# Bringing the experts' rows back through a table in DRAM in place of selection matmuls, for 12 of 16 pairs of experts

## The chip, the core and the metric

The kernel runs on one core of a Trainium2 chip. Its engines are named as in the profile: PE (TensorE, the matmuls), DVE (VectorE), ACT (ScalarE), POOL (GpSimd) and SP (SyncE, which here only issues transfers). The core's 16 DMA engines are shared by all queues. The metric is the device time of one execution in microseconds, as the median of several runs.

## The reference

Two layers of a decoder trunk, on 256 tokens of 1024 columns, all in f32. Each layer has four token mixers whose outputs are gated, projected and added to the residual, and then a hierarchical mixture of experts. This is the part that matters here:

```python
lc = (xf @ w_coarse) + b_coarse                 # 4 groups
grp = jnp.argmax(lc, axis=-1)
p_grp = jnp.take_along_axis(jax.nn.softmax(lc, axis=-1), grp[:, None], axis=-1)
lf = ((xf @ w_fine) + b_fine).reshape(N, 4, 8)  # 8 experts a group
lf = jnp.take_along_axis(lf, grp[:, None, None], axis=1)[:, 0]
top_p, top_e = lax.top_k(jax.nn.softmax(lf, axis=-1), 2)
wts = p_grp * top_p / jnp.sum(top_p, axis=-1, keepdims=True)
eid = grp[:, None] * 8 + top_e
moe = routed_experts(xf, eid, wts, w13, w2)     # sum over a token's two experts of
                                                # wts * (silu(x w1) * (x w3)) w2
x = x + g2 * moe
```

So each of the 256 tokens goes to two of 32 experts, 512 token-and-expert rows in all, and a token's result is the sum of two weighted rows and the residual. An expert's matrices are w13 (1024 x 512, w1 and w3 side by side) and w2 (256 x 1024).

## The kernel before, in words

Everything is one program for one core, two layers one after the other. All compute instructions are recorded through one helper, so they carry one line number (L253); the profile tells them apart by the names of the tiles. The order of each engine's instructions is fixed when the program is written: the mixers by a hand-made order of units (SEQ, KEYS) with a rough clock that fills TensorE's waits, the experts by the plain loop of `experts`.

Tiles in SBUF: `ring` are 8 tiles of 1 MB for weights, `pg` a pool of pages of 128 x 1024 f32 (512 KB; 29 of them, for weights too, w2 above all), `gt`, `sm` and `smb` smaller scratch, `K` the table of constants with the identity. PSUM banks are `at` (short-lived) and `mm` (long sums). The weights of the whole program are one stream of pieces in a fixed order, issued by SyncE at L320 (`advance`), as soon as `done` has given back a ring tile or a page.

A layer's experts go by pairs: 16 pairs, each expert with 64 slots for its tokens, so a pair has 128 slots, one per partition. `route` gives `rk`, for each token and expert its place among the expert's tokens. The loop over p from 0 to 15 does, for pair p:

1. `first(p)`: 32 matmuls of the pair's gathered columns (XG) with w13, then SwiGLU on ScalarE and VectorE (`swiglu`: a tanh, two VectorE operations).
2. `scatter` of pair p-1: eight matmuls `mm<-pg 128x512` of the transposed selection (ST, zeros and ones, slots by tokens) with the pair's weighted rows, which add them to the four long-lived banks `acc` (256 tokens by 1024 columns).
3. `prep_g`: gathers for the pairs to come, also by selection matmuls (`at<-pg 128x256`).
4. `hidden_t(p)`: two transposes of the hidden rows (`at<-K,gt`), copied to SBUF by ScalarE.
5. In odd pairs `prep_t` for the next two pairs: `selection_t` (four transposes `at<-K,pg`, the ST of `scatter`) and `slot_weights` (`at<-W,pg 128x4`, the weight of each slot).
6. `second(p)`: matmuls of the hidden rows with w2 (`at<-pg,gt`) into two banks, each weighted by `weighted`: VectorE multiplies by the slot's weight and the gate, and `split` makes two fp32r parts for the scatter (ScalarE copies, VectorE subtracts).

The sum `acc` is started before routing by `seeds(0)` and `seeds(1)`: each two matmuls of the identity with the residual X, in f32 (four passes), `mm<-pg,K`. After pair 15 come `more_rounds` (a branch, taken only if an expert has more than 64 tokens), the last scatter, the copy of `acc` to X, and in the last layer the output.

Of the kernel before, what the change touches and what calls it, by code (L numbers as in the profile page):

```python
# [31 lines left out]
# columns of the table of shape constants  # L32
C_ID, C_IOTA, C_EI, C_SL, C_TABLES, C_TRI, C_N = 0, 128, 192, 224, 230, 1190, 1318
# [16 lines left out]
def shape_constants():  # L50
    import numpy as np
    k = np.zeros((128, C_N), np.float32)
    tab = k[:, C_TABLES:C_TRI]
    p = np.arange(128)[:, None]
    c = np.arange(256)[None, :]
    k[:, C_ID:C_ID + 128] = np.eye(128)
    dist = 128 + p - c
    tab[:, C_DM:C_DM + 256] = np.where(dist >= 0, dist, BIG)
    tab[:, C_DW:C_DW + 256] = np.where((dist >= 0) & (dist < 128), dist, BIG)
    tab[:, C_MK:C_MK + 256] = np.where(dist >= 0, 0.0, -1e30)  # L60
    t = np.arange(S).reshape(2, 128).T
# [12 lines left out]
    k[:, C_TRI:C_TRI + 128] = np.arange(128)[:, None] < np.arange(128)[None, :]  # L74
    k[:, C_IOTA:C_IOTA + 64] = np.arange(64)[None, :]
    k[:, C_EI:C_EI + 32] = np.arange(32)[None, :]
    return k


# the order of the units of each layer before its experts  # L80
# [27 lines left out]
# the order of their weights  # L108
# [20 lines left out]
class Clock:  # L129
    '''a rough forecast, while the program is written, of when each engine gets through with what it has been given'''  # L130
# [18 lines left out]
    def known(self, a, t):  # L149
        '''the tile's content is written by t'''  # L150
# [27 lines left out]
    def cost(self, e, name, out, ins):  # L178
# [6 lines left out]
        if e == "P":  # L185
# [9 lines left out]
            # strips of the array work side by side  # L195
# [63 lines left out]
def kernel(ctx, tc, x_in, c_in, w_ada, b_ada, norm_gain, w_in, qk_gain, cmp_pe, cmp_w1, cmp_w2,  # L259
# [9 lines left out]
    ps = ctx.enter_context(tc.tile_pool(name="ps", bufs=1, space=bass.MemoryType.PSUM))  # L269
    ctx.enter_context(tc.manual_schedule())  # L270
# [70 lines left out]
    def two(key, n, src, off, row, tag="any"):  # L341
        '''rows of n columns, in one piece of the ring or in two pages'''
# [76 lines left out]
    def load_rest():  # L419
# [13 lines left out]
        A.dma_start(tri_f, consts[:, C_TRI:C_TRI + 128])  # L433

    ID = K[:, C_ID:C_ID + 128]
    one = cst.tile([128, 1], FT, name="one")
# [17 lines left out]
    def slopes(l):  # L454
        # gains of the queries, in units of each head's slope
# [14 lines left out]
    def rsqrt(ss, n, inv, eng=None):  # L470
        '''1 / sqrt(ss * inv + EPS): a guess from the exponent, a step of third order and one of Newton's'''
# [34 lines left out]
    strips = cst.tile([128, 2], FT, name="strips")  # L506
# [5 lines left out]
    four = cst.tile([128, 1], FT, name="four")  # L512
# [4 lines left out]
    def put(l, part, src):  # L517
        '''eight columns of a shift or a scale, with their bias'''
# [10 lines left out]
    def strip_columns(r, rows, p=None):  # L529
        '''the sums of some strips, as columns'''  # L530
# [5 lines left out]
    def ada_pe(l, part):  # L536
        '''1024 columns on the tensor engine: two blocks of columns by even and odd rows of 128, in four strips'''
# [35 lines left out]
    def ada_v(l, part, pool=False):  # L573
        '''1024 columns, the products by row summed on the vector engine, the rows by the tensor engine'''
# [44 lines left out]
    def gate_tile(l):  # L619
        # the bias goes in as a row  # L620
# [4 lines left out]
    def router_bias(l):  # L625
        # the router's bias carries the shift through the router's weights
# [33 lines left out]
    # the residual's rows turned to columns while their norms are worked out  # L660
# [57 lines left out]
    # where the columns go: the first and the last, the tile, its columns  # L718
# [25 lines left out]
    # the first columns: the residual times the gain's scale; the norm and the shift come in afterwards  # L744
# [94 lines left out]
    # the output projection: halves of the columns (n) by halves of the rows (f)  # L839
# [43 lines left out]
    def prep(raw, n, groups):  # L883
        '''per-head RMS normalisation of n raw heads; groups: (raw column, heads, copies, column in the result)'''
# [21 lines left out]
    def pairs(xn, col, n, dst, gain):  # L906
        '''n blocks of 128 columns, transposed, times a gain by row'''
# [10 lines left out]
    def scores(qf, kf, i):  # L918
        # the two heads of a pair may lie in different rows of the array, so each has a bank
# [7 lines left out]
    def biased(p, i, slopes, table):  # L927
        '''the scores, negated, and the negated largest of each row'''
# [29 lines left out]
    def attend(qf, kf, vf, slopes, table, take, gate=None, sinks=None):  # L958
        '''four heads by twos, each pair's output turned, as heads by tokens'''
# [47 lines left out]
        def one_pair(i):  # L1007
            # a number that is yielded: the banks that the next step takes; held: those that are read later
# [9 lines left out]
    def turned(b):  # L1018
        '''takes a branch's output for the projection'''
# [29 lines left out]
    def g_nsa(l):  # L1049
# [3 lines left out]
        # the raw keys and values of the compressed branch, twice side by side  # L1053
# [40 lines left out]
    def compressed(l, kT2, qT, gg, oa):  # L1094
        # hidden layer of the compression: keys and values, by halves of the hidden units
# [274 lines left out]
    # the engine of each part of the modulation: six parts a layer  # L1370
# [111 lines left out]
    def mixers(l):  # L1482
# [34 lines left out]
        def when():  # L1517
            '''when the next filling unit can start, None if not before something else is written'''
# [9 lines left out]
        def aside(force):  # L1528
            '''one of the units beside, if it is its turn'''
# [253 lines left out]
    def residual1(l, c0, c1, acc):  # L1783
        '''some columns of the residual, and their squares'''
# [9 lines left out]
    def router_part(l, q):  # L1794
        '''a quarter of the rows of the router's product'''
# [29 lines left out]
    def route(l, rs, lo):  # L1825
        '''group by its largest logit, two experts of it, and each token's place among its expert's tokens'''
# [3 lines left out]
        ei = K[:, C_EI:C_EI + 32]  # L1830
# [24 lines left out]
        # zeros and ones, exact in any type  # L1855
# [9 lines left out]
        # weights, off the path to the gather  # L1865
# [10 lines left out]
        def further():  # L1876
            # how many further rounds of CAP rows each pair of experts needs
# [7 lines left out]
        def weights():  # L1885
            V.tensor_reduce(den, ec, axis=AX.X, op=OP.add)
# [29 lines left out]
    def slot_weights(sel, ws, n):  # L1916
        p = at([128, n // 2, 2, 2])
# [5 lines left out]
        for e in range(2):  # L1923
            V.tensor_reduce(w[64 * e:64 * e + 64], p[64 * e:64 * e + 64, :, :, e], axis=AX.X, op=OP.add)
# [44 lines left out]
    def scatter(acc, st, ys, last):  # L1969
        for n in range(2):  # L1970
            for t in range(2):
                for j in range(2):
                    T.matmul(acc[t][n], st[:, 128 * t:128 * t + 128], ys[n][:, j], start=False, stop=last and j == 1)

    def more_rounds(l, acc):
        tot = nc.values_load(NRt[0:1, 16:17], min_val=0, max_val=3)
        with tc.If(tot > 0):
            with tc.For_i(0, NE // 2) as pi:
# [3 lines left out]
                V.tensor_copy(wsl, W[:, :, :, ds(2 * pi, 2)])  # L1982
# [32 lines left out]
    def experts(l):  # L2015
# [6 lines left out]
        # the sum of the experts starts from the residual  # L2022
        acc = {}
# [8 lines left out]
        seeds(0)  # L2032
# [22 lines left out]
        seeds(1)  # L2055

        NP = NE // 2
        SEL, ST, SW, XG = {}, {}, {}, {}
# [26 lines left out]
        def second(p, gT):  # L2085
            ys = []
            for n in range(2):
# [6 lines left out]
                ys.append(weighted(y, SW[p // 2][:, p % 2:p % 2 + 1], MOD[l, "g2"][:, 512 * n:512 * n + 512]))  # L2094
# [14 lines left out]
        for p in range(NP):  # L2109
# [7 lines left out]
            if l + 1 < DEPTH and p == NP - 1:  # L2117
                tables()
            g = first(p)
# [3 lines left out]
            else:  # L2123
                scatter(acc, ST[(p - 1) // 2][:, (p - 1) % 2], ys, False)
# [8 lines left out]
            ys = second(p, gT)  # L2133
        more_rounds(l, acc)
        scatter(acc, ST[q][:, i], ys, True)
# [72 lines left out]
```

## Time and profile before

| what | value |
|---|---|
| median of 3 runs | 1083.64 us (1081.47 to 1084.21) |
| span of the profiled execution | 1081.6 us |
| TensorE busy | 1039.9 us, 96% |
| VectorE, ScalarE, GpSimd busy | 55%, 41%, 13% |
| moved by DMA | 337.5 MB, mean 312 GB/s; written to HBM 1.05 MB |
| experts of layer 0 (first half of pair 0 to the last scatter) | about 311 to 552 us |
| experts of layer 1 | about 836 to 1076 us |

The profiled execution's span lies 2.0 us below the median of the runs. A timeline row gives the start from the span's beginning, the duration of a run of like instructions, engine, operation, tiles and count, and in brackets the idle time in front and what ended it. A duration of several matmuls includes the pipeline's tail, so the time that a group holds the engine is read from its start to the start of the next. DMA issues on SyncE are short; a long one is a row of several issues that waited for a tile in between.

### The profile page before, as it was taken

What the parts mean: (1) busy time and instruction counts of PE and PEld (TensorE: products, weight loads), DVE (VectorE), ACT (ScalarE), POOL (GpSimd) and SP (SyncE); (2) the same over time, 40 slices, a digit from 0 to 9 for tenths busy, and PEclk for the clock granted to TensorE, in tenths of its full rate; (3) what the DMA queues carried; (4) which work ended last, traced back from release to release, by engine and by line L of the source; (5) the groups of instructions that cost most, each with busy time, mean ns of one, the idle gap of its engine ahead of it and who ended that gap; (6) DMA issues with size and microseconds to landing.
All of it is one profiled execution on the core that took longest, in us unless ns stands there. A gap on an engine that the chain in (4) does not pass through costs nothing. (4 is left out here: it accounts for less than half of the span.)

```text
span 1081.6 us, 15476 instructions
## 1 busy us (share of the span) xinstructions
PE 1039.9 (96%) x5615; PEld 657.2 (61%) x5616; DVE 597.3 (55%) x1316; ACT 444.0 (41%) x1089; POOL 136.4 (13%) x273
## 2 busy tenths in 40 slices
PE   5989999999999999999999989999999999999997
PEld 3567777787854455544447867778876554555542
DVE  2656678888553333333357875986876233333332
ACT  2554857654441222222146467666444222221211
POOL 0021443320010000000001342530201000000000
PEclk8999999999999999999999999999999999999999
DMA  9977765678899999999966784556779799999991
GB/s 353 401 256 271 264 206 198 216 273 311 309 350 362 409 353 410 411 412 412 413 236 238 277 332 140 195 195 246 285 276 364 275 406 346 411 411 410 412 397 40
DMA packets 151056, 337.50 MB, mean 312 GB/s; under 512 B 13196, under 2 KB 30908, under 8 KB 150972
## 3 DMA queue, kind: packets, MB, share of 16 engines
q1 hardware_dynamic: 144166, 334.66, 82.2%
q10 hardware_dynamic: 6678, 1.77, 0.7%
q8 instruction: 46, 0.75, 0.3%
q14 instruction: 38, 0.31, 0.1%
q0 software_dynamic: 128, 0.02, 0.0%
HBM read 335.36 MB, written 1.05 MB: 311 GB/s over the span
## 5 line engine op out<-in xcount | busy, mean ns | idle before, releaser
L253 PE MATMUL mm<-pg 128*128 128x512 f32 (+4 forms) x1984 | 468.9, 388 | 8.5 <-ACT pg L253 7.1
L253 PEld LDWEIGHTS mm<-pg 128*128 128x128 f32 x1984 | 352.7, 189 | 120.7 <-issue 34.7
L253 PE MATMUL at<-ring,pg 128*64 128x512 f32 (+2 forms) x912 | 242.7, 569 | 2.4 <-POOL pg L253 2.4
L253 PE MATMUL at<-pg 128*128 128x256 f32 (+6 forms) x1192 | 226.6, 363 | 3.2 <-ACT pg L253 2.1
L253 DVE TENSOR_TENSOR pg<-ring,pg 128x512 fp32r<-128x512 f32 (+4 forms) x276 | 182.0, 695 | 68.2 <-ACT pg L253 66.2
L253 PEld LDWEIGHTS at<-pg 128*128 128x128 f32 (+3 forms) x1192 | 130.4, 167 | 71.3 <-issue 57.4
L253 ACT ACTIVATE pg<-ring 128x512 fp32r<-128x512 f32 (+4 forms) x276 | 148.7, 602 | 17.9 <-DMA rbs<-in_b_fine_dram 5.1
L253 PEld LDWEIGHTS at<-ring,pg 128*64 128x64 f32 (+2 forms) x912 | 81.1, 137 | 101.4 <-issue 88.7
L253 PE MATMUL at<-pg,gt 128*64 128x512 f32 x512 | 116.9, 598 | 2.2 <-ACT gt L253 2.1
L253 ACT ACTIVATE gt<-at 128x256 f32<-128x256 f32 x64 | 24.6, 384 | 213.6 <-PE at L253 213.6
L253 DVE SCALAR_TENSOR_TENSOR gt<-gt,at 128x256 f32<-128x256 f32 x32 | 13.5, 421 | 147.2 <-ACT gt L253 147.2
L253 ACT ACTIVATE pg<-gt 128x512 fp32r<-128x512 f32 x64 | 40.3, 629 | 115.5 <-DVE gt L253 115.5
L253 DVE SCALAR_TENSOR_TENSOR gt<-at,sm,pg 128x512 f32<-128x512 f32 x64 | 47.9, 748 | 61.8 <-PE at L253 61.8
L253 ACT ACTIVATE pg<-pg,sm 128x128 f32<-128x128 f32 (+2 forms) x168 | 70.2, 459 | 17.0 <-DVE sm L253 12.0
L253 ACT ACTIVATE pg<-at 128x512 f32<-128x512 f32 (+5 forms) x106 | 49.9, 503 | 54.9 <-PE at L253 54.7
L253 PEld LDWEIGHTS at<-pg,gt 128*64 128x64 f32 x512 | 33.9, 136 | 60.1 <-issue 52.0
L253 DVE TENSOR_TENSOR pg<-gt,pg 128x512 fp32r<-128x512 f32 x64 | 44.3, 692 | 45.8 <-ACT pg L253 45.1
L253 DVE TENSOR_SCALAR pg<-at,A,mod 128x256 f32<-128x256 f32 x64 | 31.6, 539 | 60.9 <-PE at L253 59.2
L253 PE MATMUL at<-K,pg 128*128 128x128 f32 (+1 forms) x388 | 59.6, 283 | 5.9 <-DVE pg L253 3.4
L253 PEld LDWEIGHTS at<-K,pg 128*128 128x128 f32 (+1 forms) x388 | 46.3, 143 | 20.5 <-DVE pg L253 5.7
L253 DVE SCALAR_TENSOR_TENSOR pg<-ring,cs,pg 128x1024 f32<-128x1024 f32 x44 | 58.0, 1319 | 0.1
L253 ACT ACTIVATE gt<-mm 128x512 f32<-128x512 f32 x44 | 24.5, 594 | 80.9 <-PE mm L253 80.8
(162 smaller groups left out, 676.9 us busy)
## 6 DMA issues: line engine op xcount, KB each, us to landing
pg<-in_w_dram SPq DMA_DIRECT2D x196, 512.0 KB, 11.0
ring<-in_w_dram SPq DMA_DIRECT2D x94, 1024.0 KB, 12.1
ring<-in_w_ada_dram SPq DMA_DIRECT2D x45, 1024.0 KB, 7.8
ring<-in_w_in_dram SPq DMA_DIRECT2D x33, 1024.0 KB, 4.7
ring<-in_cmp_w_dram SPq DMA_DIRECT2D x8, 1024.0 KB, 6.4
ring<-in_w_branch_dram SPq DMA_DIRECT2D x8, 1024.0 KB, 4.9
ring<-in_w_out_dram SPq DMA_DIRECT2D x8, 1024.0 KB, 5.0
ring<-in_w_in_dram SPq DMA_DIRECT2D x8, 976.0 KB
```

The costliest lines, as they stand in the source:

```text
L253: return f(*args, **kw)
```

## The change

`NSUM = 4`: only the last four pairs (12 to 15) are still summed by selection matmuls. For pairs 0 to 11 `second` weights both halves straight into one page y1 (128 slots by 1024 columns), without the split, and `put_rows` sends the page by an indirect DMA from GpSimd's queue to a table in DRAM, one of 512 rows by 1024 columns for each layer. Row 2 * token + choice belongs to a token's first or second expert. The row of each slot comes from a third part of W, which rides along in `slot_weights` (now 128x6) and is made an integer by two VectorE operations; empty slots get row 1024, which is out of bounds and dropped.

At pair 14 `fetch` reads the table back into four pages of 512 KB by GpSimd's queue, at pair 15 `gather_rows` adds the two rows of each token (four GpSimd additions) and adds them to X (two VectorE additions). The seeds now come after the second half of pair 15 and add that X to `acc`; the sum is started by the first of the scatters left, which is that of pair 12. Rows that no pair below 12 writes must be zero, so both tables are zeroed once, by two ScalarE DMAs of 2 MB (from one zeroed tile of 128x512) while the parameters are loaded. The constants lose a table of 32 columns and gain two; some small tiles share one (`few`).

```diff
+NROW, NOROW = 512, 1024
+NSUM = 4
...
+    rows_of = [dr.tile([NROW, D], FT, name=f"rows{l}") for l in range(DEPTH)]
...
+        zero = T_("gt", [128, 512])
+        G.memset(zero, 0.0)
+        for r in rows_of:
+            A.dma_start(r.rearrange("(p r) (a c) -> p (r a) c", p=128, c=512),
+                        zero[:, None, :].to_broadcast([128, 8, 512]))
...
-    W = cst.tile([128, 2, 2, NE], FR, name="W")
+    W = cst.tile([128, 2, 3, NE], FR, name="W")
...
         def weights():
+            for t in range(2):
+                V.tensor_scalar(W[:, t, 2], o12[:, t, 1], K[:, C_ROW + t:C_ROW + t + 1], None, op0=OP.add)
...
+            if rows is not None:
+                V.tensor_scalar(rows[64 * e:64 * e + 64], p[64 * e:64 * e + 64, :, 2, e], float(NOROW), None, op0=OP.add)
...
+    def put_rows(l, y, rows):
+        nc.gpsimd.indirect_dma_start(out=rows_of[l][:, :], out_offset=bass.IndirectOffsetOnAxis(ap=rows, axis=0), in_=y,
+                                     in_offset=None, bounds_check=NROW - 1, oob_is_err=False)
...
-        def seeds(t):
-            acc[t] = [mmb(), mmb()]
-            for n in range(2):
-                T.matmul(acc[t][n], ID, X[t][:, 512 * n:512 * n + 512], start=True, stop=False)
+        def fetch():
+            for t in range(2):
+                for c in range(2):
+                    back[t, c] = pg([128, D])
+                    G.dma_start(back[t, c], rows_of[l].rearrange("(t p c) d -> t c p d", t=2, c=2)[t, c])
+        def gather_rows():
+            for t in range(2):
+                for n in range(2):
+                    c = slice(512 * n, 512 * n + 512)
+                    G.tensor_tensor(back[t, 0][:, c], back[t, 0][:, c], back[t, 1][:, c], op=OP.add)
+                V.tensor_tensor(X[t], X[t], back[t, 0], op=OP.add)
+        def seeds():
+            for t in range(2):
+                for n in range(2):
+                    T.matmul(acc[t][n], ID, X[t][:, 512 * n:512 * n + 512], start=False, stop=False)
...
-            selection_t(SEL[q], ST[q], 4)
-            SW[q] = slot_weights(SEL[q], W[:, :, :, 4 * q:4 * q + 4], 4)
+            if 2 * q + 1 >= SUM:
+                selection_t(SEL[q], ST[q], 4)
+            TO[q] = T_("sm", [128, 2], I32)
+            SW[q] = slot_weights(SEL[q], W[:, :, :, 4 * q:4 * q + 4], 4, TO[q])
...
-                ys.append(weighted(y, SW[p // 2][:, p % 2:p % 2 + 1], MOD[l, "g2"][:, 512 * n:512 * n + 512]))
+                if p < SUM:
+                    V.scalar_tensor_tensor(y1[:, 512 * n:512 * n + 512], y, w, gate, op0=OP.mult, op1=OP.mult)
+                else:
+                    ys.append(weighted(y, w, gate))
+            if p < SUM:
+                put_rows(l, y1, TO[q][:, i:i + 1])
...
+            if p == SUM + 2:
+                fetch()
...
-            else:
-                scatter(acc, ST[(p - 1) // 2][:, (p - 1) % 2], ys, False)
+            elif p > SUM:
...
+                scatter(acc, ST[(p - 1) // 2][:, (p - 1) % 2], ys, p == SUM + 1, False)
+            if p == NP - 1:
+                gather_rows()
...
+        seeds()
         more_rounds(l, acc)
-        scatter(acc, ST[q][:, i], ys, True)
+        scatter(acc, ST[q][:, i], ys, False, True)
```

On TensorE, this is pair 9 of layer 0 before, from its scatter (of pair 8) to the first matmuls of pair 10; `at<-ring,pg` is `first`, `at<-pg,gt` is `second`:

```order
305 L253 MATMUL mm<-pg 128x512 x8
306 L253 MATMUL at<-pg 128x256 x8
307 L253 MATMUL at<-K,gt 128x128 x2
308 L253 MATMUL at<-K,pg 128x128 x4
309 L253 MATMUL at<-W,pg 128x4 x4
310 L253 MATMUL at<-pg,gt 64x512 x8
311 L253 MATMUL at<-ring,pg 64x512 x8
```

And the same pair now:

```order
290 L257 MATMUL at<-pg 128x256 x8
291 L257 MATMUL at<-K,gt 128x128 x2
292 L257 MATMUL at<-W,pg 128x6 x4
293 L257 MATMUL at<-pg,gt 64x512 x8
294 L257 MATMUL at<-ring,pg 64x512 x8
```

The scatter and the selection's transposes are gone, slot_weights is wider by two columns, and the hidden rows' transposes stand one gather behind the first half.

The end of layer 0's experts on TensorE before, pair 15 from the scatter of pair 14 on; `NRt` belongs to `more_rounds`:

```order
390 L253 MATMUL mm<-pg 128x512 x8
391 L253 MATMUL at<-K,gt 128x128 x2
392 L253 MATMUL at<-pg,gt 64x512 x8
393 L1976 TENSOR_LOAD NRt
394 L1977 COMPARE_AND_BRANCH
```

And now:

```order
370 L257 MATMUL mm<-pg 128x512 x8
371 L257 MATMUL at<-K,gt 128x128 x2
372 L257 MATMUL at<-pg,gt 64x512 x8
373 L257 MATMUL mm<-pg,K 128x512 x4
374 L2000 TENSOR_LOAD NRt
375 L2001 COMPARE_AND_BRANCH
```

The scatter of pair 14 stays, and the four seed matmuls stand between the second half of pair 15 and the branch.

On GpSimd, the instructions between layer 0's routing (the last small `sm` operations) and the branch after pair 15, before:

```order
93 L253 TENSOR_TENSOR sm<-smb,sm 128x8
94 L253 TENSOR_TENSOR sm<-sm 128x2
95 L1976 TENSOR_LOAD NRt
96 L1977 COMPARE_AND_BRANCH
97 L1978 COMPARE_AND_BRANCH
```

And now, with the table under its number in the program (`rows_66`):

```order
94 L257 TENSOR_TENSOR sm<-smb,sm 128x8
95 L257 TENSOR_TENSOR sm<-sm 128x2
96 L1994 DMA rows_66<-pg,sm 512x1024 x12
97 L2053 DMA pg<-rows_66 128x1024 x4
98 L257 TENSOR_TENSOR pg<-pg 128x512 x4
99 L2000 TENSOR_LOAD NRt
100 L2001 COMPARE_AND_BRANCH
```

Where the queue went from routing to the branch with nothing between, it now has the twelve puts, the four fetches and the four additions, in this order.

## Rows read from the trace of the kernel before

**Rows 1.** Page: busy time of each engine, and GpSimd's DMA queue.

```profile
PE 1039.9 (96%) x5615; PEld 657.2 (61%) x5616; DVE 597.3 (55%) x1316; ACT 444.0 (41%) x1089; POOL 136.4 (13%) x273
...
q0 software_dynamic: 128, 0.02, 0.0%
```

**Rows 2.** Stretches: length; busy of PE, PEld, DVE, ACT, POOL; clock; DMA share; GB/s.

```profile
70.00:90.00 20.00, 20.00 (x116) 13.93 (x115) 10.25 (x22) 8.49 (x21) 4.24 (x14) 1.00 1.04 373
100.00:120.00 20.00, 19.57 (x167) 13.72 (x165) 12.53 (x39) 12.33 (x47) 6.77 (x24) 1.00 0.78 286
310.00:350.00 40.00, 39.42 (x205) 18.93 (x204) 14.41 (x33) 10.14 (x21) 0.00 (x0) 1.00 0.93 347
380.00:400.00 20.00, 19.97 (x113) 11.03 (x113) 6.37 (x13) 4.83 (x10) 0.00 (x0) 1.00 0.95 334
420.00:530.00 110.00, 110.00 (x569) 54.13 (x564) 36.43 (x73) 22.73 (x45) 0.00 (x0) 1.00 1.04 411
840.00:860.00 20.00, 20.00 (x106) 9.93 (x103) 5.79 (x12) 5.44 (x11) 0.00 (x0) 1.00 0.73 253
900.00:920.00 20.00, 20.00 (x104) 10.16 (x101) 5.47 (x10) 4.34 (x9) 0.00 (x0) 1.00 0.86 322
920.00:1040.00 120.00, 120.00 (x625) 59.88 (x624) 41.02 (x80) 26.30 (x52) 0.00 (x0) 1.00 1.04 411
```

**Rows 3.** Timeline, TensorE, pairs 7 to 9: start, us, operation, count.

```profile
424.25 2.14 PE L253 MATMUL mm<-pg 128*128 128x512 f32 x8
426.22 1.10 PE L253 MATMUL at<-pg 128*128 128x256 f32 x8
427.16 0.38 PE L253 MATMUL at<-K,gt 128*128 128x128 f32 x2
427.38 0.60 PE L253 MATMUL at<-K,pg 128*128 128x128 f32 x4
427.74 0.59 PE L253 MATMUL at<-W,pg 128*128 128x4 f32 x4
...
454.27 0.98 PE L253 MATMUL mm<-pg 128*128 128x512 f32 x3
```

**Rows 4.** Timeline, SyncE's queue in both layers' experts.

```profile
413.16 1.84 SPq L320 DMA_DIRECT2D ring<-in_w_dram  x2
...
505.12 2.42 SPq L320 DMA_DIRECT2D ring<-in_w_dram  x2
...
514.77 4.82 SPq L320 DMA_DIRECT2D pg<-in_w_dram  x4
...
1039.12 4.31 SPq L320 DMA_DIRECT2D pg<-in_w_dram  x4
```

**Rows 5.** DMA issues: tile, queue, count, KB each, us to landing.

```profile
pg<-in_w_dram SPq DMA_DIRECT2D x196, 512.0 KB, 11.0
...
out_dram<-pg SPq DMA_DIRECT2D x4, 256.0 KB, 2.4
...
pg<-in_b_ada_dram POOLq DMA_DIRECT2D x4, 4.0 KB, 5.4
```

**Rows 6.** Timeline, TensorE: last second half of each layer; idle in brackets.

```profile
544.96 3.65 PE L253 MATMUL at<-pg,gt 128*64 128x512 f32 x16 [0.53 <-ACT gt L253]
...
1068.97 3.65 PE L253 MATMUL at<-pg,gt 128*64 128x512 f32 x16 [0.53 <-ACT gt L253]
```

**Rows 7.** Timeline, TensorE, first of the two seeds in layer 0.

```profile
297.24 1.88 PE L253 MATMUL mm<-pg,K 128*128 128x512 f32 x4
```

**Rows 8.** Timeline, VectorE: last step of SwiGLU in pair 7.

```profile
425.23 0.42 DVE L253 TENSOR_TENSOR gt<-gt,at 128x256 f32<-128x256 f32 x1
```

**Rows 9.** Groups of GpSimd's instructions, by form: its additions of 128x512.

```profile
L253 POOL TENSOR_TENSOR pg<-pg,gt 128x512 f32<-128x512 f32 x16 | 29.6, 1875 | 108.4 <-DVE gt L253 108.4
```

**Rows 10.** TensorE after a long idle time, and the stretch at half rate.

```profile
63.48 5.84 PE L253 MATMUL mm<-pg 128*128 128x488 f32 x18 [2.92 <-ACT pg L253]
...
65.00:68.50 3.50, 3.50 (x11) 2.84 (x9) 2.76 (x8) 3.48 (x8) 0.00 (x0) 0.51 1.14 331
```

More of the change, by code (lines that the diff above doesn't have):

```diff
@@ L30 @@
 GATE0 = 2476
-C_ID, C_IOTA, C_EI, C_SL, C_TABLES, C_TRI, C_N = 0, 128, 192, 224, 230, 1190, 1318
+C_ID, C_IOTA, C_SL, C_ROW, C_TABLES, C_TRI, C_N = 0, 128, 192, 198, 200, 1160, 1288
 C_DM, C_DW, C_MK, C_CM, C_VIS, C_COS, C_SIN = 0, 256, 512, 768, 832, 896, 928
@@ L75, in shape_constants @@
     k[:, C_IOTA:C_IOTA + 64] = np.arange(64)[None, :]
-    k[:, C_EI:C_EI + 32] = np.arange(32)[None, :]
+    k[:, C_ROW:C_ROW + 2] = 2 * t - NOROW
     return k
@@ L269 @@
     ps = ctx.enter_context(tc.tile_pool(name="ps", bufs=1, space=bass.MemoryType.PSUM))
+    dr = ctx.enter_context(tc.tile_pool(name="dr", bufs=1, space=bass.MemoryType.DRAM))
+    rows_of = [dr.tile([NROW, D], FT, name=f"rows{l}") for l in range(DEPTH)]
     ctx.enter_context(tc.manual_schedule())
@@ L433, in load_rest @@
         A.dma_start(tri_f, consts[:, C_TRI:C_TRI + 128])
+        zero = T_("gt", [128, 512])
[3 more added lines that the diff above has]
+                        zero[:, None, :].to_broadcast([128, 8, 512]))
+        M.unread.discard(zero.tensor.name)
+        M.used[zero.tensor.name] = M.t["G"] + 20.0
     ID = K[:, C_ID:C_ID + 128]
-    one = cst.tile([128, 1], FT, name="one")
+    few = cst.tile([128, 4], FT, name="few")
+    one, strips, four = few[:, 0:1], few[:, 1:3], few[:, 3:4]
     V.memset(one, 1.0)
@@ L505 @@
     MOD = {}
-    strips = cst.tile([128, 2], FT, name="strips")
     V.tensor_tensor(strips, ID[:, 0:64:32], ID[:, 64:128:32], op=OP.add)
@@ L511 @@
         V.tensor_tensor(evens[:, 32 * i:32 * i + 32], ID[:, 64 * i:64 * i + 32], ID[:, 64 * i + 32:64 * i + 64], op=OP.add)
-    four = cst.tile([128, 1], FT, name="four")
     V.tensor_tensor(four, strips[:, 0:1], strips[:, 1:2], op=OP.add)
@@ L1829, in route @@
             V.scalar_tensor_tensor(L[:, t], H["lg"][t], rs[:, t:t + 1], MOD[l, "rb"], op0=OP.mult, op1=OP.add)
-        ei = K[:, C_EI:C_EI + 32]
+        ei = K[:, C_IOTA:C_IOTA + 32]
         lf = L[:, :, 8:40].rearrange("p t (g e) -> p t g e", g=4)
@@ L1914, in selection_t, with slot_weights @@
         A.activation(st, p, AF.Copy)
-    def slot_weights(sel, ws, n):
-        p = at([128, n // 2, 2, 2])
+    def slot_weights(sel, ws, n, rows=None):
+        p = at([128, n // 2, ws.shape[2], 2])
         for i in range(n // 2):
@@ L1967, in weighted, with scatter @@
         return y
-    def scatter(acc, st, ys, last):
+    def scatter(acc, st, ys, first, last):
         for n in range(2):
@@ L1972, in scatter @@
                 for j in range(2):
-                    T.matmul(acc[t][n], st[:, 128 * t:128 * t + 128], ys[n][:, j], start=False, stop=last and j == 1)
+                    T.matmul(acc[t][n], st[:, 128 * t:128 * t + 128], ys[n][:, j], start=first and j == 0,
+                             stop=last and j == 1)
+    def put_rows(l, y, rows):
+        nc.gpsimd.indirect_dma_start(out=rows_of[l][:, :], out_offset=bass.IndirectOffsetOnAxis(ap=rows, axis=0), in_=y,
+                                     in_offset=None, bounds_check=NROW - 1, oob_is_err=False)
+        M.unread.discard(y.tensor.name)
+        M.used[y.tensor.name] = M.t["V"] + 4.0
     def more_rounds(l, acc):
@@ L1981, in more_rounds @@
                 wsl = T_("sm", [128, 2, 2, 2], FR)
-                V.tensor_copy(wsl, W[:, :, :, ds(2 * pi, 2)])
+                V.tensor_copy(wsl, W[:, :, 0:2, ds(2 * pi, 2)])
                 rounds = nc.values_load(NRt[0:1, ds(pi, 1)], min_val=0, max_val=3)
@@ L2020, in filler @@
                 units.pop(0)[1]()
-        acc = {}
-        def seeds(t):
-            acc[t] = [mmb(), mmb()]
-            for n in range(2):
-                T.matmul(acc[t][n], ID, X[t][:, 512 * n:512 * n + 512], start=True, stop=False)
+        acc, back = {}, {}
+        def fetch():
[13 more added lines that the diff above has]
+                    T.matmul(acc[t][n], ID, X[t][:, 512 * n:512 * n + 512], start=False, stop=False)
         filler(1)
         mm = router_part(l, 3)
-        seeds(0)
         rs = rstd_of(H["ss"])
@@ L2054, in experts @@
         filler(FILL)
-        seeds(1)
         NP = NE // 2
-        SEL, ST, SW, XG = {}, {}, {}, {}
+        SUM = NP - NSUM
+        SEL, ST, SW, XG, TO = {}, {}, {}, {}, {}
         def prep_sel(q):
@@ L2086, in second @@
             ys = []
+            q, i = divmod(p, 2)
+            y1 = pg([128, D]) if p < SUM else None
             for n in range(2):
@@ L2093, in second @@
                                  start=k == 0, stop=k == 1)
-                ys.append(weighted(y, SW[p // 2][:, p % 2:p % 2 + 1], MOD[l, "g2"][:, 512 * n:512 * n + 512]))
+                w, gate = SW[q][:, i:i + 1], MOD[l, "g2"][:, 512 * n:512 * n + 512]
+                if p < SUM:
[4 more added lines that the diff above has]
+                put_rows(l, y1, TO[q][:, i:i + 1])
             for k in range(2):
@@ L2122, in experts @@
                 prep_t(0)
-            else:
-                scatter(acc, ST[(p - 1) // 2][:, (p - 1) % 2], ys, False)
+            elif p > SUM:
+                if p == SUM + 1:
+                    for t in range(2):
+                        acc[t] = [mmb(), mmb()]
+                scatter(acc, ST[(p - 1) // 2][:, (p - 1) % 2], ys, p == SUM + 1, False)
+            if p == NP - 1:
+                gather_rows()
             if nxt:
```

2 lines of the change are left out of this document (1 added, 1 removed).

## The prediction

> **What bounds the kernel now.** I read the page's head first: TensorE is busy 96% of the span, and GpSimd's own DMA queue moves next to nothing, 0.02 MB in 128 packets [rows 1]. That would make TensorE the bound, but the share is a mean, so I then read the stages. In the middle of the experts two limits are met at once: over 110 us of layer 0 and 120 us of layer 1 TensorE is busy without a gap, and the 16 DMA engines are full too, at 411 GB/s [rows 2]. One pair of experts brings 6.29 MB of weights (2 x 3 matrices of 1024x256, 4 bytes each), so the stream needs 6.29 MB / 411 GB/s = 15.3 us a pair. SyncE's queue shows it: from its issue at 413.16 to that at 505.12 are six pairs, 15.33 us each [rows 4]. TensorE's own pace: the scatter in pair 7 starts at 424.25 and that in pair 9 at 454.27, so a pair takes 15.0 us [rows 3]. The engine is a hair faster than the stream and lives on a lead that the stream got before. How long is the lead at the end? The last w2 pieces are issued by 514.77 + 4.82 = 519.6 in layer 0 and 1039.12 + 4.31 = 1043.4 in layer 1 [rows 4] and land 11.0 us later [rows 5], at 530.6 and 1054.4; the last second half of a pair uses them at 544.96 and 1068.97 [rows 6]. So the weights are 14.4 and 14.6 us ahead when they end. That lead is what a faster TensorE can eat, and no more, unless the stream itself ends earlier.
>
> **What TensorE loses.** A scatter holds it 426.22 - 424.25 = 1.97 us; twelve per layer go: 23.6 us. The transposes of a selection hold it 427.74 - 427.38 = 0.36 us [rows 3]; six of eight go: 2.2. The two seeds ahead of the experts go, at most 1.88 us each, and the same matmuls come back behind the last pair [rows 7]; part of those in front stood beside routing's work on other engines. I book nothing for the two together; bounds -3.8 and +3.8.
>
> **What TensorE gets in their place.** The scatter covered SwiGLU. The first half of pair 7 ends at 424.25, VectorE's last step of SwiGLU at 425.23 + 0.42 = 425.65 [rows 8]. The gather that stays holds TensorE 427.16 - 426.22 = 0.94 us [rows 3], so the hidden rows' transposes then wait from 425.19 to 425.65 and a hop, some 0.55 us, twelve times: 6.6 (bounds 0 and 12 x 1.4, no cover). Where the selection's transposes go, slot_weights alone, 0.59 us [rows 3], stands between the hidden transposes and their use, against an idle time of 0.53 where nothing stood between [rows 6]: 0.1 us, six times, 0.6. On VectorE and ScalarE two splits a pair go and two operations on 64 rows come; both are far under half busy there [rows 2]. So TensorE alone would save 23.6 + 2.2 - 7.2 = 18.6 us a layer and need 15.0 - 18.6 / 12 = 13.5 us a pair.
>
> **What the stream makes of that.** 13.5 is less than 15.3, so TensorE catches up with the weights some eight or nine pairs in, and from there their last landing decides. About 1.5 us of lead I leave standing (a hop, and pieces that land out of step with their use; bounds 0 and 4). To be had: 12.9 and 13.1 us.
> Against it, what the table costs on the same 16 engines. A put carries a 128x1024 page, but 512 rows in 16 pairs fill only 32 of 128 slots on average; the others are out of bounds. If dropped rows move nothing, 12 x 32 x 4 KB = 1.57 MB, 3.8 us a layer. The fetch reads 2.1 MB, 5.1 us; it is let go when the second half of pair 13 has ended, so it shares with the weights of pair 15. Both at the rate of [rows 2]; the nearest price of a write is the output's, 256 KB in 2.4 us with the engines else idle [rows 5].
> In its favour, the stream has holes where it waits for pages and ring tiles that TensorE gives back, and a faster TensorE gives them back sooner. Layer 0: 310 to 350 at 347 GB/s and 380 to 400 at 334 are (64 x 40 + 77 x 20) / 411 = 10.0 us lost. Layer 1: 840 to 860 at 253 and 900 to 920 at 322 are (158 + 89) x 20 / 411 = 12.0 [rows 2]. Part of them is SyncE's limit of eight transfers under way and the first fill, not TensorE. I take less than half, 4.4 and 5.6; bounds 0 and all.
> Layer 0: 12.9 - 3.8 - 5.1 + 4.4 = 8.4 us gained. Layer 1: 13.1 - 8.9 + 5.6 = 9.8.
>
> **The waits that come.** On GpSimd twelve puts, four fetches and four additions stand in one queue, and nothing else does in this stage. The puts are serial, each waits for the landing of the one before, so each must take less than a pair. Nearest row: a GpSimd DMA of 4 KB takes 5.4 us to land [rows 5]. With a full page's 1.3 us of bytes I take 7; bounds 3 (the output's 2.4 and a hop) and 21.6 (b_ada's 128 packets are 32 a transfer [rows 1], so 0.17 us each, times 128 rows). At 7 every page comes free more than a pair before SyncE wants it. Behind the fetch stand four additions of 128x512 at 1.9 us [rows 9] and two on VectorE, some 10 us, and two pairs' time from the end of pair 13's second half, about 29 us, is there for both: hidden, if the fetch lands within 18 us. VectorE's two additions stand in front of pair 15's weighting, so a late fetch delays the end one for one; I book 0, bound 5 a layer.
> **Zeroing.** Two writes of 2.1 MB from ScalarE's queue at about 74 us, where the engines run at 373 GB/s: 10.2 us of transfer in a stretch that feeds a TensorE without gaps. From 100 us on the rate falls to 286 [rows 2], so there is slack to give it back; two of SyncE's pieces wait for these writes' landing. I take 1, bounds 0 and 10.
>
> **Sum**: 1081.6 - 8.4 - 9.8 + 1.0 = 1064.4 us for the profiled execution; the median of the runs lies 2.0 above that span (1083.6), so **1066 us**.
>
> **A rule weighed.** The nearest row on a software queue is the 5.4 us above. The Trainium skill (DMA: Bandwidth & Descriptors, Anatomy of one DMA — SWDGE (gpsimd) path) puts such a DMA at about 2.0 us plus its bytes at 436 GB/s; as an estimate by that page a put of a full page would take 3.2 us. The row for 4 KB is already above it, so the row decides, and the sum is the same by either. The same skill (SBUF — State Buffer, SBUF: two separate sides) speaks against the change: while VectorE runs certain operations from SBUF to SBUF, GpSimd can't write its descriptors; by that, rival (b) would hold. VectorE is busy 36.4 of 110 us there [rows 2]; no row here shows a put beside it.
>
> **Rivals.**
> (a) Slower: dropped rows cost their bytes. The DMA engines would carry 12 x 128 x 4 KB = 6.3 MB, 15.3 us a layer instead of 3.8. Layer 0: 12.9 - 15.3 - 5.1 + 4.4 = -3.1; layer 1: 13.1 - 20.4 + 5.6 = -1.7; with zeroing 5.8 us longer, 1089. It turns slower from 8.6 us of extra transfer a layer. For: the instruction's shape is the full page. Against: a row out of bounds has no place to be written to. 10%.
> (b) Slower, far: a put takes longer than a pair, by a blocked GpSimd or by a price per packet. At 21.6 us the last of twelve lands 259 us after the first could start; the fetch was to go 13 pairs after that, 199 us, and can be some 15 late: 45 us a layer, 1066 + 90 = 1156. It decides from (199 + 15) / 12 = 17.8 us a put. For: 0.17 us a packet. Against: 5.4 us for 4 KB must be mostly a fixed part. 6%.
> (c) Faster: writes and fetch fit beside the reads, and ten of the 22 us of holes close. Then TensorE's 18.6 a layer is all had: 1083.6 - 37 = 1047. For: the output's 256 KB in 2.4 us. Against: the engines show a share of 1.04 [rows 2], full. 13%.
> (d) Eaten: the table's bytes cost twice what the weights' do, 17.8 us a layer (single rows, writes between reads). Layer 0: 12.9 - 17.8 + 4.4 = -0.5; layer 1: 0.9; zeroing takes 1: 1084. A fall of the clock would act alike: after an idle time of 2.92 us TensorE ran at half rate (1.2 GHz) from 65.0 to 68.5 [rows 10]. The new waits of 0.5 us are shorter; the wait for weights, 15.3 - 13.5 = 1.8 us a pair if it comes in one piece, is nearer. At half rate for 3.5 us of each pair TensorE would need 1.75 more, 15.3, as much as the stream. 9%.
> The forecast itself: 62%; by itself 1053 to 1076 (holes nearly all closed, or none and zeroing dearer).
>
> **Chances.** About 3 us, 0.3%, is what a measurement of this kernel can tell. Faster: the forecast but for a sliver, and (c): 0.74. Same: (d) and the sliver: 0.10. Slower: (a) and (b): 0.16. The range reaches from (c) to just past (a): 1047 to 1090.
>
> **What would show it.** Right: SyncE's last w2 issue only some 4 us earlier after the start of a layer's experts than now, while pair 15 ends 8 to 10 earlier; TensorE with gaps behind the weights from about pair 9 on; about 411 GB/s still; some 3 MB written by GpSimd's queue and 4.2 read by it; a put under 10 us; hidden transposes idle about 0.5 behind VectorE; no long wait at the seeds; 70 to 110 us unchanged but for a us. Wrong: 12 MB or more written by GpSimd's queue (a), a put of over 17 us or SyncE waiting for GpSimd's puts (b), TensorE without gaps at 13.5 us a pair to the end (c), or a total rate well under 411 while puts run (d).

## The result, and the profile after

The changed kernel is slower: 1096.26 us median (1095.13 to 1097.02, 4 runs) against 1082.56 (1081.24 to 1084.21), ratio 1.0118 with a 95% interval of 1.009 to 1.0146. The forecast was 1066, a gain of 17; the profiled execution took 1093.5 us where the sum had 1064.4.

First the stages, from the TensorE timelines (us; the third column is experiment e1 below). "Experts" goes from the hidden transposes of pair 0 to the second half of pair 15.

| stage | before | after | e1 |
|---|---|---|---|
| start to layer 0's experts | 321.4 | 325.2 | 325.3 |
| experts, layer 0 | 223.6 | 229.1 | 222.6 |
| from there to layer 1's experts | 300.5 | 299.2 | 299.1 |
| experts, layer 1 | 223.5 | 225.7 | 218.1 |
| from there to the end | 12.6 | 14.3 | 14.1 |
| span | 1081.6 | 1093.5 | 1079.1 |

So the experts, which were to gain 8.4 and 9.8 us, lost 5.5 and 2.2. Stretches of the kernel after (length; busy of PE, PEld, DVE, ACT, POOL; clock; DMA share; GB/s):

```profile
74.00:94.00 20.00, 15.96 (x77) 12.80 (x77) 10.29 (x22) 8.17 (x21) 0.58 (x1) 0.83 1.05 381
420.00:500.00 80.00, 71.13 (x338) 29.71 (x338) 19.81 (x48) 8.29 (x19) 5.60 (x5) 0.96 1.04 396
462.00:466.00 4.00, 4.00 (x11) 1.10 (x8) 0.00 (x0) 0.00 (x0) 0.00 (x0) 0.58 1.03 393
540.00:550.00 10.00, 6.69 (x28) 1.83 (x28) 1.64 (x3) 0.63 (x1) 0.00 (x0) 1.00 1.04 397
```

The second row is the one to stop at. TensorE has gaps, as forecast, so the stream decides. The DMA engines are as full as before, a share of 1.04 [rows 2], but they move 396 GB/s, puts included, not 411. At 540 to 550 no put and no fetch runs any more, and it is still 397. SyncE's queue has the same: from one pair to the next it needs 16.65 us (four pairs from the first row to the second), 15.33 before [rows 4]:

```profile
405.05 1.79 SPq L326 DMA_DIRECT2D ring<-in_w_dram  x2
...
471.65 2.16 SPq L326 DMA_DIRECT2D ring<-in_w_dram  x2
...
536.58 4.37 SPq L326 DMA_DIRECT2D pg<-in_w_dram  x4
```

The last row ends at 540.95, 21.4 us later than its fellow before (519.6). TensorE meets each piece of weights as it lands (kernel after, end of layer 0; the idle time and what ended it stand in brackets):

```profile
537.03 2.79 PE L257 MATMUL at<-pg,gt 128*64 128x512 f32 x10 [0.70 <-DMA pg<-in_w_dram]
542.43 3.22 PE L257 MATMUL at<-ring,pg 128*64 128x512 f32 x13 [1.56 <-DMA ring<-in_w_dram]
547.83 0.64 PE L257 MATMUL at<-ring,pg 128*64 128x512 f32 x1 [1.75 <-DMA ring<-in_w_dram]
...
554.27 3.65 PE L257 MATMUL at<-pg,gt 128*64 128x512 f32 x16 [0.53 <-ACT gt L257]
```

The table's own transfers look as the forecast had them. GpSimd's queue moved 7.23 MB in 4736 packets, a put landed 6.7 us after its issue (the sum took 7), a piece of the fetch 10.2, a zeroing write 17.4:

```profile
q0 software_dynamic: 4736, 7.23, 1.8%
...
rows<-gt ACTq DMA_DIRECT2D x2, 2048.0 KB, 17.4
pg<-rows POOLq DMA_DIRECT2D x8, 512.0 KB, 10.2
...
rows<-pg,sm POOLq DMA_INDIRECT x24, 6.7
```

### The profile page after: what moved, and what is told of

It reads as the page before. It is cut to its first block, busy times and chain, and to the rows that moved or that the text cites. A ratio compares the mean times of both kernels' runs of the same rounds, so it can differ in the third digit from the quotient of the medians.

```text
span 1093.5 us, 15027 instructions
## 1 busy us (share of the span) xinstructions
PE 1015.3 (93%) x5375; PEld 621.7 (57%) x5376; DVE 573.0 (52%) x1308; ACT 406.6 (37%) x1029; POOL 176.3 (16%) x314
## 3 DMA queue, kind: packets, MB, share of 16 engines
q0 software_dynamic: 4736, 7.23, 1.8%
HBM read 339.54 MB, written 17.83 MB: 327 GB/s over the span
## 5 line engine op out<-in xcount | busy, mean ns | idle before, releaser
L257 PE MATMUL mm<-pg 128*128 128x512 f32 (+4 forms) x1792 | 418.4, 387 | 9.3 <-ACT pg L257 8.2
L257 PEld LDWEIGHTS mm<-pg 128*128 128x128 f32 x1792 | 320.0, 190 | 94.5 <-issue 18.3
L257 PE MATMUL at<-ring,pg 128*64 128x512 f32 (+2 forms) x912 | 253.2, 566 | 22.1 <-DMA ring<-in_w_dram 20.2
L257 PE MATMUL at<-pg 128*128 128x256 f32 (+6 forms) x1192 | 234.4, 369 | 6.8 <-DVE pg L257 3.5
L1994 POOL DMA_INDIRECT rows<-pg,sm x24 | 26.6, 1109 | 324.6 <-DVE pg L257 324.6
L257 DVE SCALAR_TENSOR_TENSOR pg<-at,sm,pg 128x512 f32<-128x512 f32 x48 | 36.0, 751 | 64.3 <-PE at L257 64.3
L257 ACT ACTIVATE pg<-at 128x512 f32<-128x512 f32 (+5 forms) x94 | 42.9, 491 | 48.0 <-PE at L257 47.8
L257 PE MATMUL at<-K,pg 128*128 128x128 f32 (+1 forms) x340 | 52.6, 285 | 5.9 <-DVE pg L257 3.4
L257 PEld LDWEIGHTS at<-K,pg 128*128 128x128 f32 (+1 forms) x340 | 40.8, 144 | 19.4 <-DVE pg L257 5.9
L257 POOL TENSOR_TENSOR pg<-pg,gt 128x512 f32<-128x512 f32 x16 | 29.1, 1842 | 109.4 <-DVE gt L257 109.4
```

Of the source, the lines that this page charges most:

```text
L257: return f(*args, **kw)
L1994: nc.gpsimd.indirect_dma_start(out=rows_of[l][:, :], out_offset=bass.IndirectOffsetOnAxis(ap=rows, axis=0), in_=y, in_offset=None, bounds_ ...
```

## The experiments

**What the diff also moved.** Tiles lie one behind the other in each partition, constants first, each rounded up to 32 bytes. The change made the constants K 128 bytes smaller (230 to 200 columns, 928 to 800), merged three small tiles into one (64 fewer) and made W 256 larger: 64 bytes more. So the ring and the pages, into which all weights go, begin at byte 26944 in the program and not at 26880, which is 105 x 256. Theory A: this address slows the stream. Theory B: the puts, their dropped rows or GpSimd's queue do.

e1, the changed kernel with 64 bytes of constants fewer:

```diff
+    both = [cst.tile([128, 2 * n], FT, name=f"both{n}") for n in (2, 4)]
...
-        m = cst.tile([128, 2], FT, name=f"mlg{l}")
+        m = both[0][:, 2 * l:2 * l + 2]
...
-        n = cst.tile([128, 4], FT, name=f"nsink{l}")
+        n = both[1][:, 4 * l:4 * l + 4]
```

> The changed kernel with 64 bytes per partition fewer of constants: two pairs of small tiles share one each, nothing else moves. The weights' tiles then begin at a multiple of 256 bytes in each partition, as before the change; in the changed kernel they begin 64 bytes behind one. Theory A (the address of the weights' tiles sets the rate of the stream): full stretches of the experts go back from 395 to about 411 GB/s, and the time falls from 1096 to about 1070 (the forecast of 1066 plus 4 us that zeroing took from the start). Theory B (the puts, their dropped rows or GpSimd's queue slow the stream): nothing changes, 395 GB/s and 1096 us.

e2, the kernel before with 64 bytes more (`cst.tile([128, 16], FT, name="unused")`):

> The kernel before with an unused constant tile of 64 bytes per partition, which moves the weights' tiles 64 bytes behind a multiple of 256. Theory A: the full stretch of the experts falls from 411 to about 395 GB/s; a pair then needs 15.9 us of stream against 15.0 of TensorE, 16 pairs take about 10 us of the 14 us lead, the rest of the program loses a few us where it waits for weights: 1083 to 1095. Theory B: no change, 411 GB/s and 1083.

e3 and e4, the kernel after and e1 without the line `put_rows(l, y1, ...)`:

> The changed kernel without the 24 indirect puts (the rows of pairs 0 to 11 are left out of the sum); addresses as in the changed kernel. Theory A: still about 395 GB/s in full stretches, so most of the slowness stays; the stream is spared 0.3 us a put, 1088 to 1093. Theory B: 411 GB/s and the forecast's gain or more, 1060 to 1068.

> As the aligned changed kernel, without the 24 puts (the rows of pairs 0 to 11 are left out of the sum). Both theories: 411 GB/s. Its distance to the aligned kernel with puts is what the puts cost: by the forecast's 3.8 us a layer about 7 us; if dropped rows cost their bytes about 30; if puts are hidden 0.

e12, the kernel before with 128 bytes fewer (small tiles merged as in the change and in e1):

> The kernel before with 128 bytes per partition fewer of constants (small tiles merged): the weights' tiles begin 128 bytes behind a multiple of 256, a multiple of 128. If the rate goes with multiples of 128: 411 GB/s in full stretches and 1082. If it goes with 256: 394 GB/s as when shifted by 64, 1084 to 1086.

The same stretch, 420 to 500 us, of e1, e2, e3, e4 and e12 in this order:

```profile
420.00:500.00 80.00, 74.13 (x374) 33.06 (x376) 21.66 (x52) 11.00 (x25) 5.61 (x5) 1.00 1.04 411
```

```profile
420.00:500.00 80.00, 80.00 (x414) 38.77 (x412) 27.61 (x55) 16.39 (x32) 0.00 (x0) 1.00 1.04 394
```

```profile
420.00:500.00 80.00, 74.51 (x374) 32.54 (x371) 20.67 (x50) 9.99 (x23) 0.00 (x0) 1.00 1.04 394
```

```profile
420.00:500.00 80.00, 77.31 (x402) 34.62 (x400) 24.47 (x56) 12.26 (x27) 0.00 (x0) 1.00 1.04 411
```

```profile
420.00:500.00 80.00, 80.00 (x413) 38.56 (x409) 26.83 (x53) 16.38 (x32) 0.00 (x0) 1.00 1.04 394
```

Theory A holds and B falls: the last number is 411 where the weights begin at a multiple of 256 and 394 to 396 where they don't, with puts and without, in the kernel before and after; 128 is not enough (e12). The times: e1 1085.88 (ratio to before 1.0016, 0.9996 to 1.0037), 10 us under the kernel after; e2 1086.07 (1.0018, 0.9996 to 1.004) and e12 1082.33 (1.0002, 0.998 to 1.0024); e3 1087.82 (1.004, 1.0011 to 1.0069), e4 1070.86 (0.9878, 0.9836 to 0.992). Theory A had 1070 for e1, the forecast but for zeroing; that is missed by 16 us, so the address is not all that the forecast had wrong. It also had 1084 to 1086 for e12, whose time has not moved.

Why does the same loss cost the kernel before next to nothing? In e2 the last w2 issue ends 9.6 us later than before, and the last second half starts only 2.1 us later (544.96 before, [rows 6]). Those 2.1 are the later start of the experts (323.5 against 321.4), which take 223.6 us in both, and in e12 too: the lead pays.

```profile
524.57 4.58 SPq L320 DMA_DIRECT2D pg<-in_w_dram  x4
```

```profile
547.07 3.23 PE L253 MATMUL at<-pg,gt 128*64 128x512 f32 x14 [0.53 <-ACT gt L253]
```

The changed kernel has spent that lead, so there every microsecond of stream is one of time.

What dropped rows move: without puts GpSimd's queue carried 4.21 MB (e3), so 24 puts are 3.02 MB, 0.126 MB each, 31 rows of 4 KB out of 128. And at 420 to 500 us the rate, puts included, is 411 with puts (e1) and without (e4). So in a full stretch a put takes the bytes of its valid rows, 0.31 us, and rival (a) falls.

What all puts cost is more. The stages of the experts, hidden transposes of pair 0 to second half of pair 15 as above, in us:

| experts | after | e3, no puts | e1 | e4, no puts | e5 | e8, no fetch |
|---|---|---|---|---|---|---|
| layer 0 | 229.1 | 224.3 | 222.6 | 216.7 | 223.1 | 217.6 |
| layer 1 | 225.7 | 219.8 | 218.1 | 212.5 | 218.0 | 212.4 |

Twelve puts take 5.9 and 5.6 us (e1 against e4), or 4.8 and 5.9 (after against e3), where the sum had 3.8 a layer. What they cost beyond their bytes was not followed up. The whole spans differ less (1079.1 and 1070.9, 8.2 us), because e4's profile lost 3.2 us between the layers, where no put runs. The medians say 15, with an uncertainty of about 5; e1's profiled execution is the fastest of its ten runs (1080.8 to 1088.3), e4's the slowest of its four (1069.7 to 1072.8).

**Zeroing and the fetch.** e5 takes the two DMAs out of the parameters' loading and issues them from GpSimd in the middle of layer 0's mixers, behind 50% and 65% of its units (`z_at`):

```diff
-            A.dma_start(r.rearrange("(p r) (a c) -> p (r a) c", p=128, c=512),
-                        zero[:, None, :].to_broadcast([128, 8, 512]))
...
+            if z_at and len(todo) <= z_at[0]:
...
+                G.dma_start(r.rearrange("(p r) (a c) -> p (r a) c", p=128, c=512),
+                            zero[:, None, :].to_broadcast([128, 8, 512]))
```

> The aligned changed kernel, its tables zeroed later: by two GpSimd DMAs in the middle of layer 0's mixers, where the stream had slack, not by ScalarE at 74 us. Theory A (zeroing costs where the stream is full): the start of layer 0's experts comes back by 3 to 4 us, time 4 below the aligned kernel. Rival (zeroing costs its 10 us of transfer wherever it stands, or the two fetches and puts are what is late): the same time as the aligned kernel, the loss only moves.

Measured 1081.47 (0.9997, 0.9979 to 1.0016), beside a kernel before of 1081.58; e1 had 1085.88 beside 1083.19. So e5 is 2.8 us better off than e1 against its own kernel before, which the two intervals don't separate. The start of layer 0's experts says more, since many profiles share the work ahead of it: 325.2 to 328.8 us in the four with early zeroing (after, e1, e3, e4), 320.4 to 325.9 and 322.6 on average in the seven with late zeroing (e5 to e11), 321.4 to 323.5 in the three without a table (before, e2, e12). Early zeroing costs some 3.5 us, and late zeroing nothing that shows.

There are two waits. At 74 us zeroing makes ScalarE late with its splits (kernel after: two issues on its queue, then a long idle time of TensorE, behind which it runs at half rate, clock 0.83 in the first stretch above); in e5 TensorE is busy throughout that stretch. The kernel after, ScalarE's queue and TensorE:

```profile
75.27 1.97 ACTq L443 DMA_DIRECT2D rows<-gt  x2
```

```profile
78.09 7.66 PE L257 MATMUL mm<-pg 128*128 128x488 f32 x23 [4.04 <-ACT pg L257]
```

And e5:

```profile
74.00:94.00 20.00, 20.00 (x111) 14.61 (x110) 13.58 (x28) 11.04 (x31) 1.34 (x5) 1.00 1.06 396
```

In e1 this first wait is only 1.86 us, at full rate. But a second one comes behind it: a piece of weights is late, ScalarE waits for it, VectorE for ScalarE, and TensorE for VectorE. SyncE's issue of a piece, before and in e1, then ScalarE and TensorE in e1:

```profile
83.06 0.37 SPq L320 DMA_DIRECT2D ring<-in_w_in_dram  x1
```

```profile
84.26 10.30 SPq L326 DMA_DIRECT2D ring<-in_w_in_dram  x1
```

```profile
104.83 1.67 ACT L257 ACTIVATE pg<-ring 128x512 fp32r<-128x512 f32 x3 [7.40 <-DMA ring<-in_w_in_dram]
```

```profile
108.89 0.88 PE L257 MATMUL at<-K,pg 128*128 128x128 f32 x4 [2.86 <-DVE pg L257]
```

In the kernel after the same transposes start at 108.66, behind 0.43 us of idle time; before they start at 104.44. So two kernels whose first waits differ by 2 us meet again behind the late weights: there the delay is set by the late piece, so by what zeroing does to the stream, and not by ScalarE's order. What SyncE's issue of that piece waited for is not shown.

e8 is e5 without the calls of `fetch()` and `gather_rows()`:

> As the late-zeroed kernel with 12 pairs through the table, without reading the table back and adding it (these rows are left out of the sum). Theory A: the stream is spared 5.1 us a layer, about 10 us faster than with it. Rival (the fetch is hidden behind the last pairs): the same.

1070.22 (0.9898, 0.9878 to 0.9917): the fetch costs 11.3 us by the medians, 5.6 a layer, and 5.5 and 5.6 by the stages in the table; the sum had 5.1.

**How many pairs should go through the table.** If the lead is all there is to gain, few puts do as well as many. e6 and e7 are e5 with `NSUM = 12` and `NSUM = 8`, fetched two pairs behind the last put and added two pairs later:

> As the late-zeroed kernel, but only 4 pairs a layer go through the table (12 are summed by matmuls), fetched at pair 6 and added at pair 8. Theory A (the lead of the stream is what can be gained, the fetch costs 5 of it and each put 0.35): TensorE saves 4 x 1.55 - 1.5 = 4.7 us a layer and the stream's 6.5 us fit in the lead, so about 1074 to 1077. Rival (TensorE's saving by pairs decides): a third of the gain of 12 pairs, slower than the late-zeroed kernel with 12.

> As the late-zeroed kernel with 8 pairs a layer through the table, fetched at pair 10, added at pair 12. Theory A: TensorE alone would gain 10.9 us a layer, the stream leaves 14.4 - 3 - 5.1 - 2.8 = 3.5: about 1074 to 1078, no better than with 4. Rival: between the kernels with 4 and 12 in proportion to the pairs.

Both missed: 1098.32 (1.0179, 1.0142 to 1.0216) and 1092.02 (1.0095, 1.0066 to 1.0123). The profile of e6 shows a new wait, once in each layer, of 9.95 and 7.87 us (7.61 and 12.02 in e7): GpSimd fetches into four pages and adds, VectorE writes the next gather into a page that GpSimd still holds, the hidden transposes' copy stands behind ScalarE's half of that gather, and TensorE waits for it. GpSimd, VectorE, ScalarE and TensorE of e6:

```profile
396.58 0.60 POOL L2058 DMA_DIRECT2D pg<-rows  x1 [26.79 <-PE at L257]
...
414.34 2.48 POOL L257 TENSOR_TENSOR pg<-pg 128x512 f32<-128x512 f32 x2 [3.20 <-DMA pg<-rows]
```

```profile
416.86 1.00 DVE L257 TENSOR_SCALAR pg<-at,A,mod 128x256 f32<-128x256 f32 x2 [12.35 <-POOL pg L257]
```

```profile
416.86 1.02 ACT L257 ACTIVATE pg<-at,mod,A 128x256 f32<-128x256 f32 x2 [13.26 <-POOL pg L257]
417.77 0.38 ACT L257 ACTIVATE gt<-at 128x256 f32<-128x256 f32 x1
```

```profile
418.20 2.83 PE L257 MATMUL at<-pg,gt 128*64 128x512 f32 x6 [9.95 <-ACT gt L257]
```

At pair 14 no gather is left to be written (e9's last starts at 512.34, its fetch at 516.59). So e9 and e10: `NSUM = 12` and 8 again, fetch at pair 14, addition at pair 15, as in the change.

> The late-zeroed aligned kernel with 4 pairs a layer through the table, but the fetch stays at pair 14 and the addition at pair 15. Theory A (early fetching took pages that the next pairs' gathers needed; the rest of the reckoning holds): no stall in the middle of the experts; TensorE saves 4.7 us a layer, stream and fetch stay inside the lead: 1072 to 1077. Rival (matmuls and table together are what costs, each page of the split rows holds up the stream): again above 1085.

> The same with 8 pairs a layer through the table. Theory A: the stream leaves 14.4 - 2.6 - 5.6 - 2.8 = 3.4 us a layer, less than TensorE's 10.9: 1074 to 1078. Rival (TensorE's saving by pairs decides): 1062 to 1066.

1074.28 (0.9925, 0.9895 to 0.9955) and 1076.27 (0.9935, 0.9906 to 0.9964). Both beat both kernels, the one before by 8 and 6 us, and 4 puts are no worse than 8; with 12 (e5) nothing is left. In e9 TensorE has no gap in the middle and the stream runs at 411:

```profile
420.00:500.00 80.00, 80.00 (x424) 41.37 (x424) 28.10 (x62) 18.09 (x36) 0.00 (x0) 1.00 1.04 411
```

e11 is e9 without `seeds()`; the residual is added where the sum is copied:

```diff
-        seeds()
...
+                V.tensor_tensor(X[t][:, c], acc[t][n], old[t][:, c], op=OP.add)
```

> The kernel with 4 puts and late fetch, without the seed matmuls: the residual is added by VectorE where the sum is copied out of PSUM (four additions in place of two copies on each of VectorE and ScalarE). Theory A (the seeds behind the last pair stand on the path, 3.6 us a layer): 2 to 2.5 us a layer faster than with seeds, the additions cost 1 of them: 1068 to 1073. Rival (they are hidden): the same as with them.

1075.18 (0.9924, 0.9891 to 0.9957): no difference that the runs can tell from e9, and theory A's 1068 to 1073 is missed. By the profiles the seeds' 3.6 us are mostly given back, since they fill the time in which the last pair is split: the output's issue comes 9.05 us after the start of the last second half with them and 7.6 without, 1.5 us.

## Why the prediction was wrong

Right were the bound (TensorE takes the lead and then waits for the weights), the fetch's 5.1 us a layer (5.6), dropped rows at no bytes, a put's 7 us (6.7), the hidden transposes' new wait (idle 0.4 us behind VectorE, 0.55 in the sum), and that a late fetch does not delay the end.

**The step that failed** is one that the prediction does not have: it took the stream's rate, 411 GB/s, from the kernel before and carried it through the sum. The shuffle of constants was costed at nothing, without a word. It moved every weight tile by 64 bytes and cost 4% of the rate: 14.4 us between the profiled executions after and e1, 6.5 and 7.6 of it in the two layers' experts; 10.4 by the medians. That alone turns e1, no change, into slower. Without puts, e3 against e4, the same 64 bytes cost 7.6 and 7.3 in the experts and 17.0 by the medians. None of the rivals had it. (d) had the total rate falling below 411, which happened, but laid it to the table's bytes, and e3 shows 394 without a put. The Trainium skill has a rule with this boundary (DMA: Bandwidth & Descriptors, How a descriptor splits into AXI transactions): transfers go in transactions of 256 bytes that begin at multiples of 256, and a descriptor that begins elsewhere needs more of them. The boundary agrees with e1, e2 and e12. The extra by wasted bytes would be larger at 128 than at 64 by that rule; here both run at 394. So the boundary is shown, and what makes the stream slower off it is not.

Without it the forecast would still have been too good: e1 has 1079.1 in the profile, against 1064.4. The experts were to take 215.2 and 213.7 us; in e1 they take 222.6 and 218.1, 7.4 and 4.4 more (e5 repeats it, 223.1 and 218.0). Four terms of the sum were mis-sized.
- The puts were booked at 3.8 us a layer and cost 5.9 and 5.6, the fetch at 5.1 and 5.5 and 5.6. Together that is 2.5 and 2.3 of the 7.4 and 4.4.
- The holes of the stream were to close by 4.4 and 5.6 us. What is left of the 7.4 and 4.4, 4.9 and 2.1, is what they did not give: nothing in layer 0 and some 3.5 in layer 1, if the lead is as large as the sum has it. SyncE's last w2 issues say the same. In e1 they end at 530.82 + 4.17 = 534.99 and 1047.87 + 4.51 = 1052.38 (rows below the list), 15.4 and 9.0 us later than before. Of that, 3.9 and 1.4 are the later start of the experts and 11.4 and 11.2 the table by the experiments; what remains is 0.1 and -3.6. At 840 to 860 e1 still runs at 253 GB/s, as before [rows 2]; at 900 to 920 it runs at 410 in place of 322.
- Zeroing was booked at 1 us, with 10 as the bound: the start of the experts is 3.9 late in e1, and some 3.5 by all profiles. The prediction counted on slack from 100 us on to give the bytes back; by then a piece of weights was already late, and TensorE waited for it.
- The seeds were booked as nothing on balance. Nothing that shows came back in front (the kernels with late zeroing start the experts at 322.6 on average, those without a table at 321.4 to 323.5), and 1.5 to 1.8 us a layer came behind the last pair.

SyncE's last w2 issues in e1, layer 0 and layer 1:

```profile
530.82 4.17 SPq L326 DMA_DIRECT2D pg<-in_w_dram  x4
```

```profile
1047.87 4.51 SPq L326 DMA_DIRECT2D pg<-in_w_dram  x4
```

As a sum for e1: the forecast gain of 17.2, less 7.4 and 4.4 (experts), less 2.9 (zeroing), less 3.3 (seeds), is -0.8; the profile has 2.5. The rest lies between the layers, which take 299.1 us in e1 with the seeds and 300.5 before. In the eight profiles whose instructions there are the same (after, e1, e3 to e5, e8 to e10) it takes 299.1 to 303.4, so one profile doesn't settle terms of 2 us outside the experts.

Of the rivals: (b) fell with the put's 6.7 us, (c) with the stream as the bound. The clock's part in (d) was seen, in small: in the kernel after TensorE ran at half rate for a few us behind an idle time of 2.55 us (462 to 466 above). Whether it falls is not settled by the idle time alone. At the end of e5's layer 0 it fell behind a wait of 1.41 us, the last of four within 9 us; the same 13 matmuls take 3.22 us in the kernel after, behind 1.56 (rows above):

```profile
535.14 4.91 PE L257 MATMUL at<-ring,pg 128*64 128x512 f32 x13 [1.41 <-DMA ring<-in_w_dram]
```

And e1 and e5 wait for the same piece of pair 12, 2.25 and 2.24 us; e1 keeps its clock, e5 doesn't (the stretch around that wait, e1 and then e5; the clock is the third number from the end):

```profile
480.00:500.00 20.00, 16.93 (x84) 7.16 (x82) 4.34 (x12) 2.83 (x7) 1.23 (x1) 1.00 1.05 410
```

```profile
480.00:500.00 20.00, 16.77 (x76) 6.84 (x74) 4.01 (x8) 2.69 (x6) 1.23 (x1) 0.91 1.04 411
```

Left open: why e1's runs spread by 7 us and e4's by 3 (the mean clock of each run doesn't order e1's: 1087.2 at 0.998, 1082.5 at 0.991), what a put costs beyond its bytes, and whether the ring or the pages alone carry the address effect; all moved together in every run.

## What to carry to other kernels

When two limits lie within 2% of each other, what an edit of one can gain is the other's lead, so count that first and spend as little as it takes: four pairs through the table gave what twelve could not. And before a cost is carried over from the old trace, ask what it rests on that the edit moves: a diff that resizes any tile in front of the big buffers changes their addresses, and a full stream's GB/s is the number to compare first, ahead of all stories on the new instructions.

## What the runs showed of the hardware

- Weights that land at addresses off a multiple of 256 bytes per partition: 394 GB/s against 411, for offsets of 64 and 128 alike, in a stream of 2 and 4 KB runs (after, e2, e3 and e12 against before, e1 and e4).
- An indirect write of a 128-row page with 97 rows out of bounds takes, in a full stretch, as much of the stream as its 31 valid rows do (411 GB/s with and without it), and GpSimd 1.1 us of its time; twelve of them lengthened the experts by 4.8 to 5.9 us, where their valid rows are 3.7; the page's figure of what HBM was written (17.83 MB) counts the dropped rows in full, the queue's own line (7.23 MB) does not.
- TensorE's half rate followed waits from 1.4 us (e5, at 535) to 4.0 us (after, at 78), not each time: 2.25 us in e1 and 1.86 us in e10 (at 205) left it at full rate, and 1.86 us at the same place in e9 did not.
